# One matrix inverse per lane: three 128-partition transposes around it instead of ten 32-partition ones

## Chip, core and metric

The kernel runs on one core of a Trainium2 chip. The metric is the device time of one execution in microseconds. Five engines matter: TensorE (PE in the profile, with its weight loads as PEld), VectorE (DVE), ScalarE (ACT), GpSimd (POOL) and SyncE (SP, which issues most DMAs). Each engine works through its own queue in order.

## What is computed

The reference is a stack of two blocks on 256 tokens and 256 context positions, 1024 channels wide. First block: layer 0 is an RWKV-7 mixer with 32 heads of 64, run in both directions, and layer 1 a Hyena mixer. The second block has two layers of retention, spatial gating and differential attention. The change touches layer 0 alone. Its core is this scan, once forward and once in reverse, first over the context and then over the tokens:

```python
def rwkv7_scan(r, decay, k, v, kk, a, s0, reverse):
    xs = tuple(jnp.moveaxis(t.astype(jnp.float32), 1, 0) for t in (r, decay, k, v, -kk, kk * a))

    def step(s, inp):
        r_t, w_t, k_t, v_t, a_t, b_t = inp
        sa = jnp.einsum('bhvk,bhk->bhv', s, a_t)
        s = s * w_t[:, :, None, :] + sa[..., None] * b_t[:, :, None, :] + v_t[..., None] * k_t[:, :, None, :]
        return s, jnp.einsum('bhvk,bhk->bhv', s, r_t)

    s_last, ys = lax.scan(step, s0, xs, reverse=reverse)
    return jnp.moveaxis(ys, 0, 1), s_last
```

## The kernel before

**Chunks and groups.** The scan is done in chunks of 64 positions: 4 of the context and 4 of the tokens. Within a chunk, the term with `sa` is a triangular system, solved by multiplying with the inverse of a unit triangle of 64x64. There is one triangle for each chunk, head and direction. The heads go in 8 groups of 4, so that a group has 8 chunks x 4 heads x 2 directions = 64 triangles. Direction `z` 0 or 1 takes partitions 0 to 63 or 64 to 127, and the 32 blocks (chunk, head) lie along the free dimension.

**Steps of a group.** `rwkv_prep` (L842) makes the operands `AR`, `BK` and others from the projections, mostly on VectorE, ScalarE and GpSimd. `rwkv_inverse` (L936) makes the inverses `TT`. `rwkv_chain` (L1013) then runs the 8 chunks of either direction in order. One piece of the chain is a step of one direction: a right-hand side in PSUM (`ry`), ScalarE's copy of it (`RB`, L1076), the product with `TT` (`us`), ScalarE's copy `UV` (L1081), the state's update (`us` again, `St` L1092, `SB` L1094 and L1095 on GpSimd), and y. Beside that, `operands` prepares the next step's `qk` product, which VectorE masks into `ATT` (L1045). `rwkv_readout` closes a group.

**The inverse.** L941 to L955: 64 matmuls of 64x64x64 for a group (`mm`, L953, tile `pp`) make `AB`, copied out by ScalarE in four parts (L954). A 64x64 triangle consists of two diagonal 32x32 triangles and one off-diagonal block. L963 to L968: four transposes on VectorE (`nc.vector.transpose`, each 32 partitions by 1024 elements) bring the diagonal blocks into `LA` with one whole 32x32 matrix on each partition ("lane"). `lane_inverse` (L1111) inverts 32x32 triangles lane by lane with products and sums along the free dimension (`prod`, `mZ`, L1124 and L1125), VectorE for the most part, GpSimd for two of the products. L973 to L983: six more transposes of 32 partitions, four into `TT` (L980) and two into `T1` (L982). L985 to L1011: two rounds of 32x32 matmuls (`pi`) with ScalarE's copies (`XM` L996, `TT` L1010) give the off-diagonal block.

**Order.** While the chain of group g runs, each of its 16 pieces pulls along pieces of the inverse of g+1, of the preparation of g+2, of the read-out of g-1 and of the other layers' modulations (L816 to L821). The generators yield weights and `self.tot = [40, 51]` (L711) scales them: the inverse's weights are spread over 12 of the 16 pieces. That is the order in which the instructions are written; a planner (`schedule_with_timeline_sim=True`) then orders each engine's queue by its own model of times, and places the semaphores. Group 0's preparation and inverse come before the core, beside the projections of values and gates.

**Room.** Tiles of one tag share slots. `L` has three slots (`LA`, `X`, GpSimd's products, `T1`, `XM`); `prod` has one.

Of the kernel before, what the change touches and what calls it, by code (L numbers as in the profile page):

```python
# [31 lines left out]
# ---------------------------------------------------------------- constants of the shapes alone  # L32
def shape_constants():
# [24 lines left out]
    # filter embedding and window  # L58
# [32 lines left out]
    # second block: rotary tables and distances  # L91
# [24 lines left out]
class Parts:  # L116
    """K-tiles of an operand kept in several tiles of 4"""
# [9 lines left out]
class Net:  # L127
# [29 lines left out]
    def rstd(self, dst, ss, n, eps, pool):  # L157
        """dst = (ss / n + eps) ** -0.5; all [P, m]."""
        nc = self.nc
        sh = list(ss.shape)  # L160
        v = self.t(pool, sh, "rstd_v")
        nc.vector.tensor_scalar(v, ss, 1.0 / n, eps, ALU.mult, ALU.add)  # L162
        nc.gpsimd.tensor_tensor(dst, v, self.mhalf[:, 0:1].to_broadcast(sh), ALU.pow)  # L163

# [23 lines left out]
    def banks(self, n):  # L188
        """n banks for sums; after the first layer there are two of either tag, by turns"""
        if not self.two:  # L190
            return [self.t(self.ps, [128, 512], "mm") for _ in range(n)]
        tags = "mm", "x"
        self.bturn = 1 - self.bturn
        return [self.t(self.ps, [128, 512], tags[i // 2] if n > 2 else tags[self.bturn], bufs=2) for i in range(n)]

    def gemm_half_g(self, w, col0, nk, act, toks, evac):
        """the same for 512 columns in two halves, with two tiles of tokens in a bank: evac(i, psum, columns)"""
# [23 lines left out]
    def gemm_tok_g(self, w, col0, ncol, nk, act, toks, evac, tile_major=False):  # L221
        """token-major: psum[i] = act[:, toks[i]:+128]^T @ w[:, col0:+ncol]; a generator of pieces"""
# [33 lines left out]
    def gemm_ch(self, w, col0, ncol, nk, act, t0, nt, evac, side=None, raw=None):  # L256
        """channel-major: psum[c] = w[:, col0+128c:+128]^T @ act[:, t0:t0+nt]; side: a generator moved on by a
        piece after each load; raw: the first tile of w if it is loaded already"""
# [19 lines left out]
    def matvec(self, l, w, b, cols, gate_rows, rows, raws, scol, chunks=range(6), pool=None, tag="mm", width=512):  # L278
        """rows = silu(cond) @ w + b of modulation l for two conditions, in chunks of columns; shift and scale as
        columns into cols [128, 16, 2]; the gate parts go to DRAM rows {cond: dram[1, 1024]}; a generator of pieces"""  # L280
# [5 lines left out]
        for n, j in enumerate(chunks):  # L286
# [3 lines left out]
            for q in range(2):  # L290
                raw = vs[q] if vs else load(j, q)
                # each of the 4 K-tiles in a column group of its own
# [12 lines left out]
    def matvec_end(self, l, c0, row, b, cols, gate_rows, rows, pp, tag):  # L305
        """sums the column groups' rows and adds the bias"""
# [20 lines left out]
    def norm_split(self, xt, cols, cond, gcol, H, L, dt0, pool):  # L327
        """H + L [:, k, dt0:dt0+256] = (rms_norm(x) * g * (1 + scale) + shift)^T"""
# [28 lines left out]
    def transpose_split(self, src, n, H, L, k0, dt0, ntok=2, half=False):  # L357
        """src (or half of it) token-major [128, ntok, n*128] -> H/L [:, k0+k, dt0:dt0+128*ntok]"""
# [16 lines left out]
    def residual(self, act, nk, w, streams, post, pool, done=None, side=None):  # L375
        """for every stream (old, new, gate row, first token): new = old + gate * rms_norm(act^T @ w, post);
        done(stream, tile, columns) after each part of the last; side() comes before the last K tiles"""
# [37 lines left out]
        if nk == 16:  # L415
            # the last K tiles may come late
# [22 lines left out]
        else:  # L439
            # all the weights at hand, one tile of tokens after the other  # L440
# [15 lines left out]
    def setup(self):  # L456
# [9 lines left out]
        # sums the four column groups' rows  # L466
# [3 lines left out]
    def pack_rows(self, rows, tag, pool, tmp, eng=None, ptag="mm"):  # L470
        """rows: DRAM views [n, 128]; returns [128, sum n] of their transposes"""
# [14 lines left out]
    def rwkv_project(self):  # L486
# [17 lines left out]
        # per-channel parameters as columns  # L504
# [5 lines left out]
        # silu of both blocks' conditions, [K-tile, row], the rows from 2 on zero  # L510
# [8 lines left out]
        # the tokens take the place of d until they are normalised and transposed; order: context, tokens  # L519
# [41 lines left out]
        # d = shifted - h; context: channels < 512 from the previous token, others from the next one  # L561
# [33 lines left out]
        def lerp_g(g, t0, nt, pool, tag, out, every=3):  # L595
            """out = the parts of h + mu d; gives way after each half of the channels"""
# [32 lines left out]
        # the gate of this layer's modulation, in tiles that the bottlenecks leave  # L629
# [4 lines left out]
        # k, and 1 / max(norm, 1e-12) of k * k_k per head  # L634
# [4 lines left out]
        for j in range(4):  # L639
# [9 lines left out]
            if j == 0:  # L649
                # decay and in-context-rate bottlenecks by direction, [parts x 64, tokens]  # L650
# [20 lines left out]
        # to DRAM by head; the rows lie at 32 (pair mod 4) + 2 (pair div 4) + half  # L671
# [39 lines left out]
        self.tot = [40, 51]  # L711
# [12 lines left out]
    def set(self, es):  # L724
        """room for the operands of one more group"""
# [4 lines left out]
    def operand(self, g, n, shape, tag):  # L730
        """group g's tile in the first n sets by turns"""
        return self.t(self.sets[g % n], shape, tag)

    def rwkv_open(self):
        """what the preparation needs"""
# [11 lines left out]
        # sigmoid(v) = (1 + tanh(v / 2)) / 2; k_dir = k (1 + (a - 1) k_a)  # L747
# [8 lines left out]
        # entries off the valid blocks stay zero  # L756
# [8 lines left out]
    def rwkv_core(self):  # L765
# [8 lines left out]
        # operands of the even and the odd heads of the pairs, the other heads' rows zero  # L774
# [8 lines left out]
        # the other layers' modulations, in the gaps  # L783
# [19 lines left out]
        for g in range(G):  # L803
# [7 lines left out]
            if g == G - 2:  # L811
                # the filters take the room of the third set and of the modulations
# [12 lines left out]
        # the rest goes into the gaps before the next layer  # L825
# [6 lines left out]
    def advance(self, gen, amount):  # L832
        """emit pieces of gen until their weights reach amount"""
# [8 lines left out]
    def rwkv_prep(self, g, s):  # L842
        """operands of the 4 heads of group g for both directions"""
# [3 lines left out]
        # [two copies of 64, z, w2 | a2, channel]: the product with both parts of the bottleneck at once  # L847
# [15 lines left out]
        for p in range(2):  # L863
# [6 lines left out]
            # negated normalised key direction  # L870
# [6 lines left out]
            for z in range(2):  # L877
# [16 lines left out]
                # a <- -sigmoid  # L894
# [32 lines left out]
            # bonus weights sum_k r k_dir r_k per token and head  # L927
# [8 lines left out]
    def rwkv_inverse(self, g, s):  # L936
        """inverses of the chunks' triangles"""
# [3 lines left out]
        # A_ab^T of every chunk: rows (z, s), [block (chunk, head), t]; entries outside the triangle are not read  # L941
        AB = self.t(self.abp[g % 2], [128, 32, 64], "AB")
        ABv = AB.rearrange("p (c i j) t -> p c i j t", i=2, j=2)
        for hf in range(2):
            for j in range(2):
                jr = slice(64 * j, 64 * j + 64)
                q = self.t(ps, [128, 512], "pp")
                for cc in range(4):
                    for i in range(2):
                        for z in range(2):  # L950
                            o = 128 * cc + 64 * i
                            ra = AR[z][1][jr, i, cc, 0] if hf else AR[z][0][jr, i, cc]
                            mm(q[64 * z:64 * z + 64, o:o + 64], BK[z][hf][jr, i, cc, 0], ra, True, True)  # L953
# [3 lines left out]
        # unit-lower inverses of the 32x32 diagonal blocks, one block per lane  # L957
# [4 lines left out]
        nc.gpsimd.memset(Xt[:, 0:1024:33], 1.0)  # L962
        for z in range(2):  # L963
            for hf in range(2):
                q0 = 64 * z + 32 * hf
                src = AB[q0:q0 + 32, :, 32 * hf:32 * hf + 32].rearrange("p b t -> p t b")
                dst = LA[q0:q0 + 32]
                nc.vector.transpose(dst if z == 0 else dst.rearrange("p s t -> p t s"), src)  # L968
        yield 4
        yield from self.lane_inverse(p1, LAt, Xt)  # L970

        s["TT"] = TT = self.TTs[g % 2]
# [941 lines left out]
```

## Time and profile before

| | |
|---|---|
| median of 3 runs | 2575.11 us (2574.1 to 2586.33) |
| span of the profiled execution | 2584.2 us |
| busy PE, DVE, ACT, POOL | 92%, 62%, 46%, 32% |
| layer 0's core (first chain to last) | about 404 to 1262 us |
| mean granted TensorE clock | 0.944 of full speed |

A busy share of the page is a mean over stages with different limits. The core is one stage of nearly 900 us in which neither PE nor DVE is full on the mean. It has a period of 104 to 112 us, one group, and is read period by period.

### The profile page before, as it was taken

What the parts mean: (1) busy time and instruction counts of PE and PEld (TensorE: products, weight loads), DVE (VectorE), ACT (ScalarE), POOL (GpSimd) and SP (SyncE); (2) the same over time, 40 slices, a digit from 0 to 9 for tenths busy, and PEclk for the clock granted to TensorE, in tenths of its full rate; (3) what the DMA queues carried; (4) which work ended last, traced back from release to release, by engine and by line L of the source; (5) the groups of instructions that cost most, each with busy time, mean ns of one, the idle gap of its engine ahead of it and who ended that gap; (6) DMA issues with size and microseconds to landing.
All of it is one profiled execution on the core that took longest, in us unless ns stands there. A gap on an engine that the chain in (4) does not pass through costs nothing. (4 is left out here: it accounts for less than half of the span.)

```text
span 2584.2 us, 43519 instructions
## 1 busy us (share of the span) xinstructions
PE 2377.7 (92%) x17635; PEld 1995.9 (77%) x17635; DVE 1595.8 (62%) x2238; ACT 1201.3 (46%) x2238; POOL 834.1 (32%) x800
## 2 busy tenths in 40 slices
PE   6999977788888888979899999999999999999998
PEld 4578866667676666767779998788899987888886
DVE  6564495967779687694457676653345634654464
ACT  4345464564655646545335444433235623433453
POOL 4233342554545445442112333120022111121231
PEclk9999986987888989899999999999999999999999
DMA  6546441232232332204446554332222132344333
GB/s 216 199 141 193 159 156 44 87 116 83 88 111 86 96 103 84 64 27 148 141 146 201 166 165 162 110 114 82 82 79 86 52 122 82 119 130 133 100 130 131
DMA packets 203757, 305.82 MB, mean 118 GB/s; under 512 B 12593, under 2 KB 110542, under 8 KB 203556
## 3 DMA queue, kind: packets, MB, share of 16 engines
q1 hardware_dynamic: 194528, 276.08, 33.1%
q0 software_dynamic: 6096, 19.77, 2.1%
q10 hardware_dynamic: 2932, 7.18, 0.9%
q8 instruction: 139, 2.28, 0.4%
q14 instruction: 62, 0.51, 0.1%
HBM read 281.93 MB, written 21.06 MB: 117 GB/s over the span
## 5 line engine op out<-in xcount | busy, mean ns | idle before, releaser
L155 DVE TENSOR_TENSOR wlo<-wraw,whi 128x2048 fp32r<-128x2048 f32 (+1 forms) x156 | 364.5, 2338 | 315.6 <-ACT whi L154 315.4
L154 ACT CAST whi<-wraw 128x2048 fp32r<-128x2048 f32 (+1 forms) x172 | 321.8, 1874 | 299.9 <-PE x L151 149.5
L151 PE MATMUL mm<-whi,hH 128*128 128x256 f32 (+1 forms) x944 | 303.0, 324 | 5.4 <-ACT rs_junk L399 2.3
L151 PE MATMUL mm<-wlo,hH 128*128 128x256 f32 (+1 forms) x944 | 302.2, 321 | 0.0
L151 PE MATMUL mm<-whi,hL 128*128 128x256 f32 (+1 forms) x944 | 300.8, 320 | 0.0
L151 PEld LDWEIGHTS mm<-whi,hH 128*128 128x128 f32 x944 | 179.8, 191 | 20.3 <-ACT rs_junk L399 2.8
L151 PEld LDWEIGHTS mm<-wlo,hH 128*128 128x128 f32 x944 | 180.0, 191 | 14.3 <-POOL wlo L155 0.2
L151 PEld LDWEIGHTS mm<-whi,hL 128*128 128x128 f32 x944 | 179.6, 190 | 14.2 <-DVE hL L355 0.2
L1045 DVE TENSOR_TENSOR ATT<-qk,mask 128x512 f32<-128x512 f32 (+1 forms) x128 | 70.4, 551 | 117.6 <-PE qk L151 72.0
L151 PE MATMUL x<-wlo,hH 128*128 128x512 f32 x352 | 141.4, 402 | 0.7 <-POOL wlo L155 0.7
L151 PE MATMUL x<-whi,hH 128*128 128x512 f32 x352 | 138.8, 401 | 1.9 <-ACT whi L154 1.9
L151 PE MATMUL x<-whi,hL 128*128 128x512 f32 x352 | 140.3, 401 | 0.0
L151 PE MATMUL ry<-UV,ATT 128*64 128x64 f32 x1536 | 139.5, 240 | 0.6 <-ACT UV L1081 0.6
L155 POOL TENSOR_TENSOR wlo<-wraw,whi 128x2048 fp32r<-128x2048 f32 x16 | 73.5, 4594 | 201.7 <-ACT whi L154 201.7
L151 PEld LDWEIGHTS ry<-UV,ATT 128*64 128x64 f32 x1536 | 116.2, 149 | 21.4 <-issue 6.7
L1094 POOL TENSOR_TENSOR St<-St,SB 128x256 f32<-128x256 f32 x84 | 76.0, 905 | 152.8 <-ACT St L1092 140.6
L151 PE MATMUL qk<-PD,BKx 128*128 128x256 f32 x256 | 81.9, 447 | 19.5 <-DVE ATT L1045 18.5
L1124 DVE TENSOR_TENSOR prod<-L,L 128x512 f32<-128x512 f32 (+8 forms) x88 | 96.3, 1094 | 0.9
L151 PE MATMUL us<-RB,TT 128*64 128x64 f32 x1024 | 93.0, 239 | 2.6 <-ACT RB L1076 2.4
L151 PEld LDWEIGHTS us<-RB,TT 128*64 128x64 f32 x1024 | 76.1, 149 | 22.7 <-issue 7.5
L151 PE MATMUL us<-UV,BKt 128*128 128x128 f32 x448 | 80.1, 305 | 8.0 <-ACT UV L1081 7.8
L1095 POOL TENSOR_TENSOR SB<-St,PC 128x256 f32<-128x256 f32 x98 | 72.6, 742 | 36.4 <-ACT St L1092 31.9
(562 smaller groups left out, 6451.1 us busy)
## 6 DMA issues: line engine op xcount, KB each, us to landing
wraw<-in_w_in SPq DMA_DIRECT2D x68, 1024.0 KB
wraw<-in_l_w_in SPq DMA_DIRECT2D x64, 1024.0 KB
raw<-in_w_mod SPq DMA_DIRECT2D x48, 512.0 KB
wraw<-in_w_out SPq DMA_DIRECT2D x24, 1024.0 KB
raw<-in_ada_w SPq DMA_DIRECT2D x24, 512.0 KB
wraw<-in_w_branch_out SPq DMA_DIRECT2D x12, 1024.0 KB
UV<-vD SPq DMA_DIRECT2D x128, 64.0 KB
lH<-in_ada_w SPq DMA_DIRECT2D x5, 1024.0 KB
```

The source lines that it names most:

```text
L151: return self.nc.tensor.matmul(out, lhsT, rhs, start=start, stop=stop)
L154: self.nc.scalar.copy(hi, src)
L155: (eng or self.nc.vector).tensor_tensor(lo, src, hi.bitcast(F32), ALU.subtract)
L1045: nc.vector.tensor_tensor(at.rearrange("p i j a t -> p (i j) (a t)"), q[:, 0:256 * na].rearrange("p (h n) -> p h n", h=4), mk, ALU.mult)
L1094: nc.gpsimd.tensor_tensor(tmp, tmp, SB[z][step % 2], ALU.add)
L1095: nc.gpsimd.tensor_tensor(SB[z][1 - step % 2], tmp, pc, ALU.mult)
L1124: eng.tensor_tensor(pr, a, b, ALU.mult)
```

## The change

Three edits in `rwkv_inverse`, and one number beside it (most other lines of the full diff only drop comments).

- The matmuls that make `AB` are split and rearranged, so that for both directions and both halves the diagonal block stands in columns 0 to 31 and the off-diagonal one in columns 32 to 63, with rows and columns exchanged for direction 1. One matmul of a chunk, head and direction becomes two (direction 0) or three (direction 1): 160 for a group instead of 64, each with 32 columns of weights.
- One transpose of 128 partitions replaces four of 32 ahead of `lane_inverse`.
- Two transposes of 128 partitions (`XT[0]` into a slot of `L`, `XT[1]` into the slot of `prod`) replace six of 32 behind it. ScalarE copies the diagonal blocks from them into `TT` with four copies of 32 partitions by 1024 elements. The `pi` matmuls read `XT` in the place of `T1` and of the diagonal blocks of `TT`.
- The yields' weights sum to 43.2 instead of 46.2, and the total they are scaled by is 46 instead of 51.

```diff
-        self.tot = [40, 51]
+        self.tot = [40, 46]
...
-                            ra = AR[z][1][jr, i, cc, 0] if hf else AR[z][0][jr, i, cc]
-                            mm(q[64 * z:64 * z + 64, o:o + 64], BK[z][hf][jr, i, cc, 0], ra, True, True)
+                            a = AR[z][1][jr, i, cc, 0] if hf else AR[z][0][jr, i, cc]
+                            b = BK[z][hf][jr, i, cc, 0]
+                            lo, hi = slice(0, 32), slice(32, 64)
+                            r0, r1 = q[64 * z:64 * z + 32], q[64 * z + 32:64 * z + 64]
+                            if z == 0:
+                                mm(r0[:, o:o + 64], b[:, lo], a, True, True)
+                                mm(r1[:, o:o + 64].rearrange("p (x y) -> p x y", y=32), b[:, hi], a.rearrange("p (x y) -> p x y", y=32)[:, ::-1], True, True)
+                            else:
+                                mm(r0[:, o:o + 64], a[:, lo], b, True, True)
+                                mm(r1[:, o:o + 32], a[:, hi], b[:, hi], True, True)
+                                mm(r1[:, o + 32:o + 64], b[:, hi], a[:, lo], True, True)
...
-        for z in range(2):
-            for hf in range(2):
-                q0 = 64 * z + 32 * hf
-                src = AB[q0:q0 + 32, :, 32 * hf:32 * hf + 32].rearrange("p b t -> p t b")
-                dst = LA[q0:q0 + 32]
-                nc.vector.transpose(dst if z == 0 else dst.rearrange("p s t -> p t s"), src)
-        yield 4
+        nc.vector.transpose(LA, AB[:, :, 0:32].rearrange("p b t -> p t b"))
+        yield 2
         yield from self.lane_inverse(p1, LAt, Xt)
...
-        T1 = self.t(p1, [128, 1056], "L", bufs=3)[:, 0:1024].rearrange("p (a b) -> p a b", b=32)
+        XT = []
+        for n, src in enumerate((X, X.rearrange("p a b -> p b a"))):
+            x = self.t(p1, [128, 1056], "L", bufs=3)[:, 0:1024] if n == 0 else self.t(p1, [128, 1024], "prod")
+            x = x.rearrange("p (b s) -> p b s", s=32)
+            nc.vector.transpose(x.rearrange("p b s -> p s b"), src)
+            XT.append(x)
+            yield 2
         for z in range(2):
             for hf in range(2):
                 q0 = 64 * z + 32 * hf
-                rows = X[q0:q0 + 32]                      # z = 0: (t, s); z = 1: (s, t)
-                alt = rows.rearrange("p a b -> p b a")
-                dst = TT[q0:q0 + 32, :, 32 * hf:32 * hf + 32].rearrange("p b t -> p t b")
-                nc.vector.transpose(dst, rows if z == 0 else alt)
-                if hf == z:
-                    nc.vector.transpose(T1[q0:q0 + 32].rearrange("p b s -> p s b"), alt if z == 0 else rows)
-            yield 3
+                nc.scalar.copy(TT[q0:q0 + 32, :, 32 * hf:32 * hf + 32], XT[z][q0:q0 + 32])
+        yield 1
...
-                    mm(q[b0:b0 + 32, 32 * j:32 * j + 32], AB[a0:a0 + 32, b, b0 - 64 * z:b0 - 64 * z + 32], T1[a0:a0 + 32, b, :], True, True)
+                    mm(q[b0:b0 + 32, 32 * j:32 * j + 32], AB[a0:a0 + 32, b, 32:64], XT[1 - z][a0:a0 + 32, b, :], True, True)
...
-                    mm(q[a0:a0 + 32, 32 * j:32 * j + 32], XM[b0:b0 + 32, b, :], TT[b0:b0 + 32, b, bt:bt + 32], True, True)
+                    mm(q[a0:a0 + 32, 32 * j:32 * j + 32], XM[b0:b0 + 32, b, :], XT[z][b0:b0 + 32, b, :], True, True)
```

## Rows read from the trace of the kernel before

**Rows 1.** The page, part 1: busy us, share of the span, instructions.
```profile
PE 2377.7 (92%) x17635; PEld 1995.9 (77%) x17635; DVE 1595.8 (62%) x2238; ACT 1201.3 (46%) x2238; POOL 834.1 (32%) x800
```

**Rows 2.** Stretches: us; busy PE, PEld, DVE, ACT, POOL (instructions); clock, DMA, GB/s.
```profile
388.00:444.00 56.00, 44.55 (x527) 39.42 (x526) 28.05 (x33) 26.01 (x58) 15.04 (x18) 0.58 0.10 31
444.00:556.00 112.00, 93.65 (x1096) 74.73 (x1096) 91.23 (x118) 67.37 (x161) 57.33 (x63) 0.94 0.33 103
556.00:668.00 112.00, 98.07 (x1019) 76.78 (x1019) 81.81 (x110) 59.07 (x143) 55.13 (x59) 0.82 0.30 93
884.00:988.00 104.00, 86.47 (x988) 68.82 (x989) 81.68 (x113) 58.74 (x141) 52.79 (x59) 0.90 0.29 91
1092.00:1164.00 72.00, 58.64 (x548) 46.97 (x548) 65.18 (x79) 32.26 (x88) 37.32 (x35) 0.94 0.11 33
1262.00:2584.20 1322.20, 1278.03 (x7828) 1133.22 (x7828) 710.03 (x1119) 543.05 (x857) 295.42 (x219) 0.98 0.37 122
```

**Rows 3.** The same view, two periods cut in two, a third's first part.
```profile
444.00:516.00 72.00, 55.78 (x499) 42.88 (x498) 70.30 (x85) 40.10 (x97) 38.30 (x41) 0.93 0.29 93
516.00:556.00 40.00, 37.87 (x598) 31.85 (x599) 20.93 (x34) 27.27 (x64) 19.02 (x23) 0.96 0.41 120
556.00:628.00 72.00, 58.07 (x502) 42.68 (x502) 71.38 (x93) 38.75 (x92) 42.46 (x44) 0.87 0.34 105
628.00:668.00 40.00, 40.00 (x521) 34.10 (x520) 10.43 (x18) 20.32 (x51) 12.67 (x15) 0.72 0.25 71
884.00:956.00 72.00, 54.48 (x485) 41.44 (x486) 71.51 (x88) 39.10 (x92) 41.27 (x45) 0.92 0.25 80
```

**Rows 4.** Timeline of DVE in one period: start, us, instruction, [idle before, releaser].
```profile
549.50 8.31 DVE L968 STREAM_TRANSPOSE L<-AB 32x1024 f32<-32x1024 f32 x4 [2.30 <-ACT AB L954]
...
612.09 1.98 DVE L980 STREAM_TRANSPOSE TT<-L 32x1024 f32<-32x1024 f32 x1
...
615.98 5.85 DVE L980 STREAM_TRANSPOSE TT<-L 32x1024 f32<-32x1024 f32 x3
621.73 1.86 DVE L982 STREAM_TRANSPOSE L<-L 32x1024 f32<-32x1024 f32 x1
```

**Rows 5.** Groups by form, DVE, 300 to 1264: count | busy us, mean ns | idle before.
```profile
L968 DVE STREAM_TRANSPOSE L<-AB 32x1024 f32<-32x1024 f32 x32 | 66.3, 2073 | 5.3 <-ACT AB L954 4.8
L980 DVE STREAM_TRANSPOSE TT<-L 32x1024 f32<-32x1024 f32 x32 | 64.4, 2011 | 0.6
...
L982 DVE STREAM_TRANSPOSE L<-L 32x1024 f32<-32x1024 f32 x16 | 30.9, 1930 | 0.0
```

**Rows 6.** Who PE waited for, 444 to 1164: total us, times, longest.
```profile
PE qk L1050 <- DVE ATT L1045: 21.1, 11, 4.1
PE qk L151 <- DVE ATT L1045: 19.3, 12, 2.9
PE pi L151 <- DVE L L982: 16.5, 8, 3.9
```

**Rows 7.** Timeline of PE: the inverse's matmuls.
```profile
403.68 1.91 PE L151 MATMUL pi<-L,AB 32*32 32x32 f32 x32 [5.61 <-DVE L L982]
...
521.40 2.11 PE L151 MATMUL pi<-L,AB 32*32 32x32 f32 x64
...
627.68 3.43 PE L151 MATMUL pi<-L,AB 32*32 32x32 f32 x64
```

**Rows 8.** Timeline of PE: small matmuls in a row (the last cut at four).
```profile
538.00 1.15 PE L151 MATMUL pp<-ARc,BKc 64*64 64x64 f32 x32 [0.64 <-ACT mv L301]
...
540.83 0.63 PE L151 MATMUL ry<-UV,ATT 128*64 128x64 f32 x8
...
590.88 0.42 PE L151 MATMUL pp<-raw,scol 128*32 128x256 f32 x4
```

**Rows 9.** ACT: two copies by form, and the timeline behind the first `pi` matmuls.
```profile
L954 ACT COPY AB<-pp 128x512 f32<-128x512 f32 x32 | 18.7, 585 | 18.0 <-PE pp L151 17.9
...
L1010 ACT COPY TT<-pi 32x512 f32<-32x512 f32 x32 | 18.4, 576 | 23.4 <-PE pi L151 23.2
...
625.59 1.16 ACT L996 COPY L<-pi 32x512 f32<-32x512 f32 x2 [4.32 <-PE pi L151]
```

More of the change, by code (lines that the diff above doesn't have):

```diff
@@ L962, in rwkv_inverse @@
         nc.gpsimd.memset(Xt[:, 0:1024:33], 1.0)
+        nc.vector.transpose(LA, AB[:, :, 0:32].rearrange("p b t -> p t b"))
+        yield 2
+        yield from self.lane_inverse(p1, LAt, Xt)
+        s["TT"] = TT = self.TTs[g % 2]
+        XT = []
[5 more added lines that the diff above has]
+            yield 2
         for z in range(2):
@@ L965, in rwkv_inverse @@
                 q0 = 64 * z + 32 * hf
-                src = AB[q0:q0 + 32, :, 32 * hf:32 * hf + 32].rearrange("p b t -> p t b")
-                dst = LA[q0:q0 + 32]
-                nc.vector.transpose(dst if z == 0 else dst.rearrange("p s t -> p t s"), src)
-        yield 4
-        yield from self.lane_inverse(p1, LAt, Xt)
-        s["TT"] = TT = self.TTs[g % 2]
-        T1 = self.t(p1, [128, 1056], "L", bufs=3)[:, 0:1024].rearrange("p (a b) -> p a b", b=32)
-        for z in range(2):
-            for hf in range(2):
-                q0 = 64 * z + 32 * hf
-                rows = X[q0:q0 + 32]
-                alt = rows.rearrange("p a b -> p b a")
-                dst = TT[q0:q0 + 32, :, 32 * hf:32 * hf + 32].rearrange("p b t -> p t b")
-                nc.vector.transpose(dst, rows if z == 0 else alt)
-                if hf == z:
-                    nc.vector.transpose(T1[q0:q0 + 32].rearrange("p b s -> p s b"), alt if z == 0 else rows)
-            yield 3
+                nc.scalar.copy(TT[q0:q0 + 32, :, 32 * hf:32 * hf + 32], XT[z][q0:q0 + 32])
+        yield 1
         XM = self.t(p1, [128, 1056], "L", bufs=3)[:, 0:1024].rearrange("p (a b) -> p a b", b=32)
@@ L1002, in rwkv_inverse @@
                 b0 = 64 * z + 32 * (1 - z)
-                bt = b0 - 64 * z
                 for j in range(16):
                     b = 16 * hb + j
-                    mm(q[a0:a0 + 32, 32 * j:32 * j + 32], XM[b0:b0 + 32, b, :], TT[b0:b0 + 32, b, bt:bt + 32], True, True)
+                    mm(q[a0:a0 + 32, 32 * j:32 * j + 32], XM[b0:b0 + 32, b, :], XT[z][b0:b0 + 32, b, :], True, True)
             for z in range(2):
```

## The prediction

> **What bounds the kernel now.** I read the page first [rows 1]: PE 92% busy, DVE 62%. By that mean DVE looks free and a change that gives PE more instructions looks bad. The stretches tell more. Behind 1262 us PE is busy for 1278 of 1322 us [rows 2]; nothing of the change runs there, so that half stays. Layer 0's core is another matter: its periods of 104 to 112 us have PE at 83 to 88% and DVE at 73 to 81%, neither full. Cutting periods in two shows why [rows 3]. In the first 72 us DVE is full (70.3, 71.4, 71.5 of 72) and PE is busy for 55.8, 58.1 and 54.5, so it idles for 14 to 18 us. In the other 40 us PE is full (37.9, 40.0) and DVE half idle or more. Two engines bound the core by turns. The first part begins with the inverse's four transposes and ends with the other six [rows 4]; the lane inverse, the next group's preparation and the chain's masks lie between. The second holds the `pi` matmuls, the end of one chain, the start of the next, and the matmuls for the next `AB`.
>
> The periods close a loop: `TT` lets the next chain begin, the next `AB` is made beside that chain's first pieces, its transposes wait for it (2.30 us idle ahead of them [rows 4]), and the lane inverse and six transposes lead to `pi` and the next `TT`. All ten transposes lie in the part that DVE sets. PE's waits agree: 21.1 + 19.3 us for DVE's masks and 16.5 us for the last transposes [rows 6].
>
> **Part 1, transposes.** A group has 4 x 2.073 + 4 x 2.011 + 2 x 1.930 = 20.2 us of them now [rows 5]. Three of 128 partitions follow. No row shows a transpose of 128 partitions. From above: four quarters one after the other, 4 x 2.02 = 8.1 us each. From below: the same 1024 elements on each partition as now, about 2.02 us; less than that is excluded, since the length in elements is the same. I take 2.02, because on ACT copies of 32x512 and 128x512 take 0.576 and 0.585 us [rows 9]: there time goes by elements, not by partitions, and that is the nearest comparison. So 3 x 2.02 = 6.1 and DVE gets back 14.1 us a group: 6.2 ahead of the lane inverse, 7.9 behind it.
>
> The Trainium skill, "Vector Engine (DVE) Microarchitecture Reference", section 3.8, puts a 32x32 reorder array ahead of each bank of 32 channels and says that it sustains one element per cycle and lane. The first half is for 2.02 us and no run here shows it. The second, with 0.96 GHz from "VectorE: DVE Perf Modes" (Specifications), would make 1.07 us for 1024 elements (an estimate); the rows show 1.93 to 2.07, so the measurement decides. By the page's rate three would be 3.2 us, 2.9 us a group more than I count.
>
> **Part 2, matmuls of AB.** 64 now run as 32 in 1.15 us, some 30 ns each at full clock [rows 8]: two column groups at a time, 60 ns for a pair. A pair becomes a set of five in four column groups of 32. Four matmuls in four column groups take 0.42 us together [rows 8], so groups of 32 do run side by side; then a set lasts as long as its longest column group. One matmul of 64 columns takes 0.63 / 8, less the tail, about 58 ns; two of 32 columns in one group take 2 x 32 = 64 (64 `pi` in 2.11 us [rows 7]). 64 instead of 60 ns x 32 sets is 0.1 us a group. From above: no overlap, 3 x 58 + 2 x 32 = 238 ns, 5.7 us a group. Between: no long row of small matmuls shows less than 30 ns a start, and 5 x 30 = 150 ns would be 2.9 us a group. A gain is excluded: no column group streams fewer columns than now. I take 0.1, since the four side by side have the new shape of weights. Eight groups: 1 us; 23 or 46 at the bounds. They lie in the part that PE sets, so all of it would count.
>
> The Trainium skill, "TensorEngine Tiling (Array Packing)", section Instruction Overhead, speaks against this split: each matmul costs some 60 cycles however short it is, and a dimension already small should not be cut. At full clock that is 25 ns (an estimate), 125 for a set, 2.1 us a group and 17 in all.
>
> **Part 3, copies into TT.** Four ACT copies of 32x1024 a group. From above twice a 32x512 [rows 9], 1.15 us; from below one, 0.58. I take 1.1, elements setting the time: 4.4 us a group on ACT. They queue from the first `XT` on, ahead of the copies of `pi` (L996) and among the chain's copies. `pi` reads `XT` and doesn't wait for them; the next chain needs `TT`, but its off-diagonal copies come later anyway. Their cover is the 4.32 us in which ACT waited for `pi` [rows 9]; without it up to 4.4 us a group come onto the path. I count 0.1, for both.
>
> **Part 4, slots and weights.** `XT[1]` holds the only `prod` slot until the second `pi` round. The next lane inverse, DVE's next user, stands behind the next `AB` and its transposes: from 538.00, the first of those matmuls, to 557.81, the end of the transposes [rows 4, 8], that is 20 us of cover; without it DVE would stop at its first product with the masks queued behind. `L` keeps its count of tiles. The weights end the inverse at 43.2 / 46 x 12 = 11.3 instead of 46.2 / 51 x 12 = 10.9 of 16 pieces, 0.4 x 7 = 2.8 us later in the written order, nothing where data sets the start, as at 549.50. No DMA moves.
>
> **The sum.** For a steady group: PE's work in the first part stays at (55.8 + 58.1 + 54.5) / 3 = 56.1 us. Without 14.1 us the part would be 57.9, with PE at 97%. I don't believe that, since the chain's steps pass through ACT and POOL. The fullest whole period has PE at 98.07 / 112 = 88% [rows 2]. With 88% the part is 56.1 / 0.88 = 63.8: a gain of 8.2, less 0.2 for parts 2 and 3, so 8.0. What stalls next is PE waiting for the chain's copies and GpSimd's state. Seven such groups: 56 us. Group 0's inverse comes ahead of the first chain; there PE waits 5.61 us at a time for the last transposes [rows 7] and is 80% busy at a clock of 0.58 [rows 2], so nearly all comes back: 12 of 14.1. Together 68 us, from 2584.2 to 2516 for the profiled execution; that one is 9 us above the median, so 2575.1 - 68 = 2507. Own range 2483 to 2539 (PE in that part at 93% or at 82%).
>
> **Rivals.**
> 1. *All of it and the clock too.* 8 x 14.1 = 113 us come back: 2462. Behind the transposes `pi` ran at half speed, 64 in 3.43 against 2.11 us [rows 7], after PE had waited; 628 to 668 had a clock of 0.72, so 22 of 40 us at half [rows 3]. With shorter waits some 5 us a group more: 2425. Against it: PE would need 97% or more. Chance 0.15, most of it between 2460 and 2480.
> 2. *Spacing.* PE starts no small matmul each 30 ns or faster in the long run (the Trainium skill's overhead, above, says nearly the same). Then 2507 + 23 = 2530. For: no row below 30. Against: four in 0.42 us. Chance 0.10.
> 3. *PE and ACT take it back.* PE cannot work denser in the first part because its gaps are the chain's latency. Then only PE's idle share there, 22% of 14.1 = 3.1 us a group, comes back: 12 + 22 = 34, 2541; with the spacing or half the copies' cover lost 2564. For: ACT and GpSimd stand in every step. Against: 57 us of PE's waits name DVE [rows 6]. Chance 0.15.
> 4. *Slower.* The transpose of 128 partitions passes its quarters one after the other, on DVE at either end of the lane inverse: 3 x 8.1 = 24.2 against 20.2 us, 4 us a group, 32 in all: 2607. It decides from 20.2 / 3 = 6.7 us for one. Chance 0.06. Then the change would not do what it says.
> 5. *Another order.* The planner, with other lengths, puts long VectorE instructions ahead of the masks: 4.4 us a group lost instead of won, 2590 and more. Chance 0.04.
>
> **How the numbers follow.** Forecast 0.50, rivals 0.15, 0.10, 0.15, 0.06, 0.04. About 0.5%, 13 us, is what a measurement tells from no change: faster is below 2562. Faster 0.50 + 0.15 + 0.10 + 0.09 = 0.84; same 0.06 (the upper end of rival 3); slower 0.10. The range from 2462 to 2560 leaves out some of rival 1, the end of rival 3, and rivals 4 and 5.
>
> **What would show it.** Right: 24 transposes of some 2 us; DVE-full parts of 60 to 66 instead of 72 us with PE near 88%; sets of five in 60 to 70 ns; the stretch behind the core unchanged. Wrong: transposes over 6 us; `AB` matmuls of 32 sets in 5 us or more for a group; ACT's copies of `pi` queued behind the new copies; PE's idle time in the DVE part now named after ACT or GpSimd.

## The result, and the profile after

The changed kernel takes 2556.3 us (median of eight executions) where the kernel before, measured again beside it, takes 2576.9: ratio 0.9893, interval 0.9866 to 0.9921. That is 27 us faster, between 20 and 35. Forecast were 68, so the sign and the range held and the size was two and a half times too large. In this document a difference of one point in the ratio stands for 25.8 us.

First, part 1 of the page of the kernel after (busy us, share of the span, instructions):

```profile
span 2557.6 us, 46534 instructions
PE 2366.6 (93%) x19171; PEld 1992.6 (78%) x19171; DVE 1508.1 (59%) x2182; ACT 1232.6 (48%) x2270; POOL 831.7 (33%) x800
```

Against [rows 1], DVE is busy 87.7 us less, though the transposes alone give back 114 (161.6 us in [rows 5], 47.6 below): something else on DVE grew by 26 us. ACT has 31 us more. The groups of the inverse by form (count | busy us, mean ns | idle before them, and what ended it), layer 0 of the kernel after:

```profile
L984 DVE STREAM_TRANSPOSE prod<-L 128x1024 f32<-128x1024 f32 x8 | 16.0, 1999 | 0.0
L974 DVE STREAM_TRANSPOSE L<-AB 128x1024 f32<-128x1024 f32 x8 | 15.8, 1971 | 9.6 <-ACT AB L965 9.6
L984 DVE STREAM_TRANSPOSE L<-L 128x1024 f32<-128x1024 f32 x8 | 15.8, 1971 | 0.1
L990 ACT COPY TT<-L 32x1024 f32<-32x1024 f32 x16 | 16.7, 1046 | 6.3 <-DVE L L984 6.2
L990 ACT COPY TT<-prod 32x1024 f32<-32x1024 f32 x16 | 16.6, 1040 | 0.2
```

A transpose of 128 partitions takes what one of 32 took, 1.97 to 2.00 us. A copy takes 1.04. Both are close to the values taken in the prediction, 2.02 and 1.1. So neither was mis-sized, and the missing time is not in their durations. Where it is not saved is seen from the period. The next rows give the first transposes of each group: before (four a group; the last group's set is the second row, from DVE's timeline) and after (one a group), with first and last start.

```profile
L968 DVE STREAM_TRANSPOSE L<-AB x28: 1933/2050/2196, 441.6 to 1101.0; 32x1024 f32<-32x1024 f32 x28
...
1094.89 8.23 DVE L968 STREAM_TRANSPOSE L<-AB 32x1024 f32<-32x1024 f32 x4 [1.26 <-ACT AB L954]
```

```profile
L974 DVE STREAM_TRANSPOSE L<-AB x7: 1910/1969/2018, 431.4 to 1074.2; 128x1024 f32<-128x1024 f32 x7
```

Group 0's part gave back 441.6 - 431.4 = 10.2 us, where 12 were forecast. The six periods between first and last set went from (1094.9 - 441.6) / 6 = 108.9 to (1074.2 - 431.4) / 6 = 107.1 us: 1.8 a group instead of 8.0 (a second profile of the kernel after, 430.0 to 1065.2, has 105.9, so 3.0). The shortfall is in the steady groups.

The stretches of the kernel after, as in [rows 2, 3] (us; busy PE, PEld, DVE, ACT, POOL; clock, DMA, GB/s): two periods cut in two, a third's first part, and what lies behind the core:

```profile
433.00:484.00 51.00, 41.86 (x321) 30.93 (x321) 48.79 (x64) 28.14 (x68) 28.34 (x27) 0.87 0.27 85
484.00:540.00 56.00, 51.23 (x949) 42.66 (x949) 25.62 (x47) 38.88 (x89) 27.35 (x35) 0.95 0.41 126
540.00:594.00 54.00, 36.97 (x272) 29.02 (x272) 52.01 (x64) 25.46 (x58) 26.64 (x25) 0.82 0.20 61
594.00:653.00 59.00, 55.70 (x956) 44.96 (x955) 24.84 (x43) 41.44 (x98) 27.08 (x36) 0.92 0.42 124
653.00:712.00 59.00, 46.80 (x338) 35.23 (x338) 56.13 (x69) 32.52 (x75) 34.09 (x34) 0.83 0.24 70
...
1240.00:2557.60 1317.60, 1274.21 (x7826) 1130.20 (x7826) 709.48 (x1118) 543.12 (x857) 294.74 (x219) 0.98 0.38 123
```

The parts in which DVE is full did get shorter, 51 to 59 us instead of 72; the forecast was 63.8. But PE is busy for only 82%, 68% and 79% of them, 77% together, where it had been 78% in [rows 3] and the forecast was 88%. PE did not get denser beside a full DVE: its busy share there did not rise. The work that it did not do there (42, 37 and 47 us instead of 56) came in the parts that PE fills, which grew from 40 to 56 and 59 us. The whole period has PE where it was, at 82 to 87%. Behind the core PE is busy for 1274 of 1318 us; nothing changed there, as forecast.

Who PE waited for in the core of the kernel after, 433 to 1153 (total us, times, longest), beside [rows 6]:

```profile
PE qk L1057 <- DVE ATT L1052: 22.9, 12, 4.9
PE qk L151 <- DVE ATT L1052: 21.7, 7, 6.1
PE ry L151 <- POOL SB L1102: 19.3, 18, 3.2
...
PE pi L151 <- DVE prod L984: 2.8, 3, 1.8
```

The wait for the last transposes went from 16.5 to 2.8 us. The wait for the masks, 21.1 + 19.3 = 40.4 us before, is 44.6 after: the freed time on DVE did not reach it. The wait for GpSimd's state stands third with 19.3 (13.3 before).

### The profile page after: what moved, and what is told of

Same layout as the page of the kernel before. It is cut to its first block, busy times and chain, and to the rows that moved or that the text cites. A ratio compares the mean times of both kernels' runs of the same rounds, so it can differ in the third digit from the quotient of the medians.

```text
span 2557.6 us, 46534 instructions
## 1 busy us (share of the span) xinstructions
PE 2366.6 (93%) x19171; PEld 1992.6 (78%) x19171; DVE 1508.1 (59%) x2182; ACT 1232.6 (48%) x2270; POOL 831.7 (33%) x800
## 5 line engine op out<-in xcount | busy, mean ns | idle before, releaser
L1102 POOL TENSOR_TENSOR SB<-St,PC 128x256 f32<-128x256 f32 x98 | 81.6, 833 | 17.2 <-ACT St L1099 13.3
L1083 ACT COPY RB<-ry 64x256 f32<-64x256 f32 x128 | 46.7, 365 | 82.7 <-PE ry L151 81.0
```

What stands on the lines that cost most here:

```text
L1083: nc.scalar.copy(rhs[zr], ry[0:64, 0:256])
L1102: nc.gpsimd.tensor_tensor(SB[z][1 - step % 2], tmp, pc, ALU.mult)
```

## Experiments

Ratios are to the kernel before, with 95% intervals. Differences between two changed kernels are taken from their ratios, their bounds from both intervals. Where nothing else is said, the edit is made in the kernel after.

**The same kernel again, and the old total.** One run repeats the kernel after; the other puts the total of the weights back:

```diff
-        self.tot = [40, 46]
+        self.tot = [40, 51]
```

> The changed kernel again, unaltered, beside the next three on one chip. Both theories: a ratio of 0.989, within 0.986 to 0.993 of the kernel before.

> The changed kernel with the old total of the weights, 51 in the place of 46, so that the inverse is written earlier beside the chain. Theory A (in the changed kernel the chain of a group follows on the chain before at once, its last UV copy to the next first one 0 to 3 us, and TT is ready 10 to 15 us too early; the chain and TensorE set the pace, the time of VectorE no longer does): an inverse that is written earlier gains nothing, 2550 to 2565. Theory C (the planner's order gave the gain away, and 46 is part of that): over 10 us of difference either way, below 2545 or above 2570.

Measured: 0.9905 (0.9875 to 0.9935) and 0.9918 (0.9884 to 0.9952). The gain repeats, and the total does not make it or spoil it.

**DVE's time given back to it.** The transposes are written several times, four of the first and three each of the other two: ten a group, as before.

```diff
-        nc.vector.transpose(LA, AB[:, :, 0:32].rearrange("p b t -> p t b"))
+        for _ in range(4):
+            nc.vector.transpose(LA, AB[:, :, 0:32].rearrange("p b t -> p t b"))
...
-            nc.vector.transpose(x.rearrange("p b s -> p s b"), src)
+            for _ in range(3):
+                nc.vector.transpose(x.rearrange("p b s -> p s b"), src)
```

> The changed kernel with each transposition done again, the first one four times, the two others three times each: ten transposes a group as before, 14 us a group of VectorE time put back, all else as changed. Theory A (what was gained is the part of VectorE's time that the chain did not cover, and the new matmuls and copies cost nothing): back to the time of before, 2570 to 2585. Theory B (VectorE's time was worth some 60 us, and the 160 matmuls and the four copies took 40 of it back): above the time of before by what they cost, 2600 or more.

Measured: 1.0147 (1.0092 to 1.0202). This splits the change in two. Without the saved DVE time it is 38 us slower than before (24 to 52): that is what all the rest of it costs, in the order that the planner chose for this run. The saved DVE time is worth the difference to the kernel after, 65 us (49 to 81), with the same reservation. The prediction had 69 for it (7 x 8.2 + 12) and about 1.5 for the rest.

**One end of it alone.** The first transpose written four times (the first edit above; 5.9 us a group, 47 in all), and the two behind the lane inverse left out:

```diff
-        for n, src in enumerate((X, X.rearrange("p a b -> p b a"))):
...
+        for n in range(2):
+            XT.append(X)
```

> The changed kernel with the transposition ahead of the lane inverse done four times: 3 x 1.97 = 5.9 us a group of VectorE put back, 47 us in all. Theory B (a microsecond of VectorE is worth 0.4 to 0.6 on the whole way between the kernels): 19 to 28 us slower than the changed kernel, ratio 0.997 to 1.001. Theory K (a knee: near the changed kernel the chain sets the pace, and VectorE's time is free): within 8 us of the changed kernel, ratio 0.987 to 0.993.

> The changed kernel without the two transpositions behind the lane inverse; the matrices are used as they lie, so that layer 0's recurrence is computed with wrong inverses. 2 x 2.0 = 4 us a group of VectorE fewer, 32 us in all, and pi starts 4 us earlier behind the lane inverse. Theory B: 13 to 19 us faster than the changed kernel, ratio 0.982 to 0.985. Theory K: within 8 us, ratio 0.987 to 0.993.

Measured: 1.0042 (1.0011 to 1.0072), 38 us more than the kernel after for 47 us of DVE (28 to 49), above both theories; and 0.9847 (0.9798 to 0.9895), 12 us less for 32 (between 27 less and 3 more). So transposes added to DVE cost 0.8 us per us here and 65 / 111 = 0.6 with all ten. What further time taken off DVE would bring is not settled by the second run.

**In what form the time comes.** The core of six runs, one profiled execution of each, from 400 us to the end of the last chain (us; busy PE, PEld, DVE, ACT, POOL; clock, DMA, GB/s): the kernel before, the kernel after, all transposes repeated, the first one four times, and two runs told below, the split matmuls alone in the kernel before and the kernel after without its four copies:

```profile
400.00:1261.00 861.00, 748.49 (x8013) 594.29 (x8013) 632.84 (x844) 470.85 (x1128) 385.55 (x415) 0.88 0.28 87
400.00:1238.00 838.00, 733.44 (x9229) 586.72 (x9227) 553.50 (x788) 492.42 (x1146) 387.28 (x412) 0.89 0.29 90
400.00:1304.00 904.00, 775.62 (x9367) 623.05 (x9366) 623.47 (x840) 501.73 (x1158) 394.00 (x414) 0.85 0.27 83
400.00:1269.00 869.00, 768.14 (x9325) 607.71 (x9324) 574.67 (x811) 496.83 (x1155) 392.92 (x412) 0.86 0.28 87
400.00:1291.00 891.00, 775.84 (x9357) 617.53 (x9358) 637.25 (x845) 472.11 (x1130) 389.64 (x415) 0.85 0.28 85
400.00:1219.00 819.00, 716.51 (x9192) 572.85 (x9191) 552.32 (x789) 464.57 (x1120) 391.66 (x412) 0.91 0.30 92
```

What PE waits is the length less its busy time: 113 us before, 105 after. With all transposes repeated it is 128, 24 more than after; the other 42 of the 66 us are PE busy for longer at a lower granted clock. With the first transpose four times PE waits 101 us, no more than after: all 31 us are busy time. The split (30 us longer in this execution, the longest of its ten) adds 27 us of busy time and 3 of waiting; leaving out the copies takes off 17 and 2. Busy time multiplied by the clock is 652 to 661 us in all six, so the matmuls' work hardly differs; how much of it ran at the lower of TensorE's two levels does. The clock of whole executions says the same: 0.930 to 0.943 in the ten with the first transpose four times, 0.944 to 0.955 in the eight of the kernel after. What made the clock fall is not shown by any run here.

**The split matmuls alone, in the kernel before.** Weights of 32 columns, 160 for a group; transposes, slots and copies as before:

```diff
-                            mm(q[64 * z:64 * z + 64, o:o + 64], BK[z][hf][jr, i, cc, 0], ra, True, True)
+                            mm(r0[:, o:o + 64], b[:, lo], ra, True, True)
+                            if z == 0:
+                                mm(r1[:, o:o + 64], b[:, hi], ra, True, True)
+                            else:
+                                mm(r1[:, o + 32:o + 64], b[:, hi], ra[:, hi], True, True)
+                                mm(r1[:, o:o + 32], b[:, hi], ra[:, lo], True, True)
```

> The kernel before with its 64 matmuls for AB split into 160 of 32 columns of weights, in the same five-in-a-set pattern as in the change, the layout of AB and all else as before. Priced by the trace of the changed kernel (80 matmuls in 1.22 us against 32 in 1.15): theory A 0.1 us a group, no difference, 2570 to 2585. Theory B: 17 to 46 us slower, 2594 to 2623.

Measured: 1.0045 (1.0011 to 1.0079), 12 us slower (3 to 20). Its rows on PE's timeline (start, us), half a group at half and at full clock:

```profile
543.20 1.93 PE L151 MATMUL pp<-ARc,BKc 64*32 64x64 f32 x80
...
664.86 1.22 PE L151 MATMUL pp<-ARc,BKc 64*32 64x64 f32 x80
```

80 matmuls in 1.22 us at full clock, against 32 in 1.15 [rows 8]: 15 ns each, 0.14 us a group, 1.1 us in all. Sets of five do run side by side, and rival 2's spacing of 30 ns is out. So of the 12 us, which lie between the two theories, the matmuls themselves are one. The rows above show the rest as a lower clock. That it comes from the order into which the planner puts 96 more instructions is likely and not shown; the next two runs show how much another order can be.

**Order alone, in the kernel before.** No instruction differs; the weights are scaled otherwise, so that pieces are written in other places.

```diff
-        self.tot = [40, 51]
+        self.tot = [40, 46]
```

```diff
-        self.tot = [40, 51]
+        self.tot = [44, 51]
```

> The kernel before with the total 46 in the place of 51: every instruction and every duration as before, the written order of the inverse against the chain later. It shows how much the planner's order alone moves the time. Theory C (the order's scatter is as large as the 12 and 16 us put down to matmuls and copies): over 10 us either way. Theories A and B: within 8 us of before.

> The kernel before with the preparation's total 44 in the place of 40: every instruction as before, another written order. A second sample of what the order alone does, beside +0.3 points from the inverse's total. Theory C (the 0.45 points of the split matmuls are order): 0.4 points or more either way. Theory B (they are the matmuls): within 0.3 points of 1.

Measured: 1.0027 (0.9997 to 1.0056) and 1.0068 (1.0037 to 1.0098): 7 (not clear of zero) and 18 us slower with the same instructions. The 12 us of the split lie within what another order does. Whether the split has a price beyond it stays open.

**The four copies left out.**

```diff
-        for z in range(2):
-            for hf in range(2):
-                q0 = 64 * z + 32 * hf
-                nc.scalar.copy(TT[q0:q0 + 32, :, 32 * hf:32 * hf + 32], XT[z][q0:q0 + 32])
```

> The changed kernel without ScalarE's four copies of the diagonal blocks into TT, so that this part of TT stays zero and the recurrence of layer 0 is computed with half of the inverse only. 4 x 1.04 us of ScalarE a group fall away. Theory A: hidden behind waits for TensorE, 0 to 5 us faster, 2551 to 2557. Theory B: they stand in the chain's queue, 4 us a group come back, 20 to 35 us faster, 2520 to 2537.

Measured: 0.9832 (0.9776 to 0.9889), 16 us less than the kernel after (0 to 32). Taken out of the version with the state on VectorE (below) they bring 12 us (1 to 23):

> The changed kernel with the state's update on VectorE and without ScalarE's four copies into TT (part of TT stays zero, layer 0's recurrence is computed with half of the inverse). With the state on GpSimd their removal brought 0.6 points. Theory B (ScalarE's queue in the chain: each us of it costs): again 0.5 points or more, ratio 0.972 to 0.977. Theory C (that was another order of the planner): ratio 0.979 to 0.985.

Measured: 0.9766 (0.9736 to 0.9796), against 0.9812. The two agree on some 14 us, 1.7 a group, where the prediction counted 0.1. But leaving out instructions also changes the order, which alone moved the kernel before by 7 and 18 us, so 14 us is not shown to be the copies' own price. ACT's timeline of the kernel after shows the place (start, us, instruction):

```profile
592.07 2.10 ACT L990 COPY TT<-L 32x1024 f32<-32x1024 f32 x2
594.20 0.72 ACT L891 ACTIVATE F<-F,one 128x512 f32<-128x512 f32 x1
594.82 0.35 ACT L1099 COPY St<-us 128x256 f32<-128x256 f32 x1
595.08 0.37 ACT L1059 COPY BKt<-qk 128x256 f32<-128x256 f32 x1
595.47 2.09 ACT L990 COPY TT<-prod 32x1024 f32<-32x1024 f32 x2
597.59 0.37 ACT L1115 COPY Y<-ry 64x256 f32<-64x256 f32 x1
597.98 0.37 ACT L1088 COPY UV<-us 64x256 f32<-64x256 f32 x1
598.37 0.69 ACT L889 ACTIVATE a<-pp,wah 128x512 f32<-128x512 f32 x1
599.09 1.17 ACT L1004 COPY L<-pi 32x512 f32<-32x512 f32 x2
```

None of these rows has idle time ahead of it. The running chain's `St` stands behind the first pair of copies, its `UV` behind the second, the `pi` copies behind both. The copies did fill the time in which ACT had waited for `pi` (36.1 us in the core before, 8.8 after), but the chain's copies come through the same queue: between two steps of a chain ACT must be free when `us` is done. Without the copies the same place runs so:

```profile
587.24 0.36 ACT L1095 COPY St<-us 128x256 f32<-128x256 f32 x1
587.50 0.39 ACT L1055 COPY BKt<-qk 128x256 f32<-128x256 f32 x1
...
588.53 0.37 ACT L1111 COPY Y<-ry 64x256 f32<-64x256 f32 x1
588.92 0.37 ACT L1084 COPY UV<-us 64x256 f32<-64x256 f32 x1
```

From `St` to `UV` it takes 1.7 us instead of 3.2. So the delay of the chain is seen. How it becomes time is not the same in the two runs: here PE waits only 2 us less in the whole core, while in the version with the state on VectorE leaving the copies out took 12 us off PE's waiting (86 to 73).

**The copies on GpSimd** instead of ScalarE:

```diff
-                nc.scalar.copy(TT[q0:q0 + 32, :, 32 * hf:32 * hf + 32], XT[z][q0:q0 + 32])
+                nc.gpsimd.tensor_copy(TT[q0:q0 + 32, :, 32 * hf:32 * hf + 32], XT[z][q0:q0 + 32])
```

> The changed kernel with the four copies of the diagonal blocks on GpSimd instead of ScalarE. Theory B (the copies cost 16 us because they stand in ScalarE's queue ahead of the chain's copies): most of it comes back, 2540 to 2550, ratio 0.983 to 0.987, as without them, unless GpSimd's state update waits behind them. Theory A (the copies cost nothing, what their removal showed is another order): as the changed kernel, 2552 to 2565, or above.

Measured: 1.0178 (1.0152 to 1.0204), 73 us worse than on ScalarE, which neither theory told. GpSimd is the emptiest of the engines by the page, and a worse place than ScalarE. Why it costs so much was not taken apart; the four copies themselves take 1.2 us each there, 4.8 us a group.

**The state on VectorE.** If GpSimd's state is what PE waits for next, and DVE now has room, the two should be exchanged. The chain already has the other branch for the last group; it is used for all:

```diff
-                    if g < 7:
+                    if g < 0:
```

> The changed kernel with the state's update of all groups on VectorE (two instructions of some 0.42 and 0.46 us that read PSUM) instead of one ScalarE copy (0.37) and two GpSimd instructions (0.97 and 0.84): the chain of a step gets 1.3 us shorter, VectorE gets 12.3 us a group more, nearly what the transposes gave back, ScalarE 5.2 less. Theory A (the chain's latency now sets the period): up to 7 x 1.3 = 9 us a group less, 2490 to 2535, ratio 0.965 to 0.982. Theory B (a microsecond of VectorE in a group is still worth 0.58, as the repeated transposes showed, and the chain's latency is hidden behind the other direction's work): 12.3 x 0.58 x 7 = 50 us more, less 10 to 20 for ScalarE: 2580 to 2600, ratio 1.00 to 1.01.

> The kernel before with the state's update on VectorE in all groups, as in the run before on the changed kernel, where that brought 0.9 points. Theory A (before, VectorE and the chain's latency are both full; only the change made the room that the shorter chain needs): 12.3 us a group more on a full VectorE eats the gain, ratio 0.995 to 1.015. Theory D (the chain's latency alone sets the pace, before as after): the same 0.9 points, ratio 0.988 to 0.994.

Measured: in the kernel after 0.9812 (0.9781 to 0.9842), 21 us less than the change alone (10 to 32); in the kernel before 1.0335 (1.0299 to 1.0371), 86 us more, beyond both theories. The same edit has opposite signs, and the change decides which. PE's waits of the kernel before with it, 444 to 1200, and then of the kernel after with it, 433 to 1140:

```profile
PE pi L151 <- DVE L L982: 36.0, 9, 6.3
PE ry L151 <- DVE SB L1101: 30.4, 17, 4.1
```

```profile
PE ry L151 <- DVE SB L1108: 20.1, 17, 3.5
PE qk L1057 <- DVE ATT L1052: 11.3, 14, 1.6
PE qk L151 <- DVE ATT L1052: 8.4, 6, 4.2
```

Before, on an engine without room, the `pi` wait doubles (16.5 to 36.0 us) and the state's wait grows as well (13.3 to 30.4). After, the masks' wait falls from 44.6 to 19.7 us although DVE has more instructions. With the copies on VectorE as well (`nc.vector.tensor_copy` in their line):

> The changed kernel with the state's update and the four copies into TT on VectorE. ScalarE loses 4.2 us a group more, VectorE gets four copies of 32x1024, 0.6 to 1.1 us each. Theory B: ScalarE's part is worth 12 to 16 us, VectorE's 2.4 to 4.4 us a group at 0.5 cost 8 to 16: between 0.977 and 0.983 of the kernel before. Theory K (VectorE's time is free by now): 0.975 to 0.979.

Measured: 0.9799 (0.9738 to 0.9861), not to be told from the 0.9812. The two are the best versions found that compute the whole inverse, some 2% below the kernel before.

**The inverse spread over 15 instead of 12 of the 16 pieces**, in the kernel after and with the state on VectorE:

```diff
-                side.append([self.rwkv_inverse(g + 1, st[g + 1]), tot[1], 0, 12])
+                side.append([self.rwkv_inverse(g + 1, st[g + 1]), tot[1], 0, 15])
```

> The changed kernel with the inverse's pieces spread over 15 of the chain's 16 pieces instead of 12. Theory A (TT comes 10 to 15 us before it is needed, the inverse is off the loop): VectorE's work is spread more evenly, the masks wait less, 0 to 15 us faster than the changed kernel, ratio 0.984 to 0.990. If the inverse is still what the next chain waits for: later by up to 3 pieces of 6.7 us in a group, slower than the changed kernel, ratio 0.995 or more.

> The changed kernel with the state's update on VectorE and the inverse over 15 pieces. Theory A: in the run with the state on VectorE, TT came 6 us ahead of its use (620 against 625 us), so there is little left to give: within 8 us of that run, ratio 0.978 to 0.985. If the inverse comes onto the loop: 0.988 or more.

Measured: 0.9958 (0.9935 to 0.998) and 0.988 (0.9846 to 0.9913): 17 us worse both times. A later inverse is no gain. That fits a `TT` without time to spare, but 17 us is also what another order alone has moved.

## Why the prediction was right or wrong

*What bounds the kernel.* Right for the kernel before: DVE and PE bound the core by turns, and the stretch behind the core is untouched. The part that DVE fills got shorter by 13 to 21 us, about all that the transposes gave back.

*The step that failed* is the sum's step from DVE's part to the period. It kept PE's work in that part at 56.1 us and let PE do it at 88% instead of 78%, so that 8.2 of 14.1 us would come back. Measured are 77%, as dense as before, and 42, 37 and 47 us of work; the rest of the work moved into the other part. PE's waiting in the core fell by 8 us, from 113 to 105, where the forecast had 57 in the seven steady groups. A steady group gained 1.8 us (3.0 in the second profile).

*Rival 3* had this: PE does not get denser there, and only its idle share of the freed time comes back, 3.1 us a group and 34 in all. Measured are 27, and its time, 2541 to 2564, came true. The repeated transposes bear out its price as well: for 111 us put back on DVE PE waited 24 us more, a fifth. They cost 65 because PE's busy time grew at a lower clock, and that the rival does not price. Its reason, the chain's latency, is not shown by itself; that the state on VectorE, a shorter chain, brought 21 us, and that PE waits 86 us in its core instead of 105, speaks for it.

*Part 1 and its conversion.* The durations were right: 1.97 to 2.00 us a transpose against 2.02. Group 0 gave 10.2 us against 12. The 65 us lie near the 69 of the sum by luck: the sum priced PE's waiting, and 42 of the 66 us in the rows are clock. Rival 4, quartered transposes, is out by the durations. Rival 1's gain did not come; its clock moved both ways, to 0.87, 0.82 and 0.83 from 0.93, 0.87 and 0.92 where DVE is full, and to 0.95 and 0.92 from 0.96 and 0.72 where PE is. Rival 5, another order, did not come as it was told (no loss), but order as a cost did; its 2590 does not follow from 4.4 us a group, which make 31 us in seven groups, or 2606.

*Parts 2 and 3* at 0.2 us a group together were the other mis-sized term. Against that stand 38 us (24 to 52) for everything but the saved DVE time.
- Part 3: the durations were right (4 x 1.04 against 4.4 us), the cover was not. The prediction set 4.4 us of copies against 4.32 us of ACT's waiting for `pi`, found the room exactly full, and then counted it as free; its own bound was 4.4 us a group. The copies stand ahead of the chain's and of the `pi` copies, a sign that it had named for being wrong. Leaving them out measured 14 us, 1.7 a group, which lies within what order moves.
- Part 2's own price was right (0.14 us a group against 0.1). That 96 more instructions a group may move the order was not priced. The split alone measured 12 us (3 to 20), and a changed order without any changed instruction 7 and 18.
- The other 12 of the 38 us are not assigned. The slots of part 4 and the order of the finished change are in them; no run separates those. The weights' total is not the cause: with 51 in the place of 46 the ratio is the same.

No term of the sum was for the clock. With the transposes repeated PE is busy for 27 us more than in the kernel before and waits 16 more. Whether the order, the copies or the split lowers the clock stays open.

*What stalls next.* The prediction named the chain's copies and GpSimd's state. The rows show both: the copies above, the state with 19.3 us. It missed that the masks' wait would stay (40.4 to 44.6 us). They were most of the 57 us that the prediction held against rival 3; that a wait names an engine did not mean that time freed on the engine would reach that wait.

*The range* reached to 2560 through rival 3 and held; the forecast's own range, 2483 to 2539, did not. Its lower bound on PE's density, 82%, was above the 78% that its own rows showed. The chance of 0.15 for rival 3 was too low for that.

## What to carry to other kernels

When a full engine gets shorter, do not let the other engine get denser beside it without a reason: take the density that the rows show, and count as gain only its idle share of the freed time. Split a measured difference into the other engine's waiting and its busy time with the granted clock beside it; here several runs differed mostly in the second. When work moves from a full engine to one with gaps, ask of each gap which chain step it belongs to: a gap as long as the work may be no cover if the next link of a latency chain comes through the same queue. Price the order too: under a planner, a change of weights alone moved this kernel by 0.7% once and by 0.3%, not clear of zero, another time, so an edit "worth nothing" carries an uncertainty of about that. And once a bottleneck engine has room, try again what was put elsewhere to relieve it: the state's update lost 3.4% on VectorE before the change and won 0.8% after it.

## What the runs showed of the hardware

VectorE's instructions grew while its work shrank. One line by form, in layer 0 of the kernels before, after, and after with the state on VectorE (count | busy us, mean ns | idle before):

```profile
L906 DVE TENSOR_TENSOR kd<-kd,K 128x512 f32<-128x512 f32 x28 | 24.2, 864 | 1.3 <-ACT kd L893 1.3
```

```profile
L906 DVE TENSOR_TENSOR kd<-kd,K 128x512 f32<-128x512 f32 x28 | 35.3, 1262 | 1.7 <-ACT kd L893 1.7
```

```profile
L906 DVE TENSOR_TENSOR kd<-kd,K 128x512 f32<-128x512 f32 x28 | 23.1, 824 | 2.7 <-ACT kd L893 2.6
```

The same instruction with the same operands differs by half in the mean. The timelines of DVE and POOL in the kernel after show one that took 3.38 us, and that of the version with the state on VectorE one that took 0.68:

```profile
569.95 3.38 DVE L906 TENSOR_TENSOR kd<-kd,K 128x512 f32<-128x512 f32 x1
...
569.90 2.89 POOL L1131 TENSOR_TENSOR L<-L,mZ 128x1024 f32<-128x1024 f32 x1 [2.29 <-DVE mZ L1132]
```

```profile
560.31 0.68 DVE L906 TENSOR_TENSOR kd<-kd,K 128x512 f32<-128x512 f32 x1
```

GpSimd's product began 0.05 us ahead of `kd` and ended at 572.79; `kd` ended 0.54 us later, close to its own length. It looks like waiting, and counts as busy. The Trainium skill, "SBUF — State Buffer", section "SBUF: two separate sides", says that a VectorE operation with two SBUF inputs and a GpSimd operation that reads SBUF share a port pair under an exclusive lock, held for the whole instruction by whoever starts first; these rows agree. So do the others of this line: 14 of its 32 products in the kernel after took over 0.9 us, with GpSimd busy beside them for 1.5 of their 1.8 us on the mean; beside the 18 others, of 0.7 us, it was busy for 0.14. The page of the version with the state on VectorE, which leaves GpSimd less work, fits too:

```profile
PE 2354.2 (93%) x19171; PEld 1983.2 (79%) x19171; DVE 1525.0 (60%) x2364; ACT 1205.8 (48%) x2172; POOL 687.8 (27%) x618
```

GpSimd gave up 144 us, and DVE took 182 instructions more, 90 us by their rows less some 11 that the last group had anyway; yet DVE's busy time rose by 17 us only. The durations of all its other instructions together fell by some 46 us; the rest is overlap of instructions that follow each other. The lock would also be a reason for the 26 us by which the rest of DVE grew under the change, which was not tested by itself. It is no reason for the 38 us of everything but the saved DVE time: in the run with the transposes repeated the growth is gone. The page there:

```profile
PE 2400.3 (91%) x19171; PEld 2020.6 (77%) x19171; DVE 1588.3 (61%) x2238; ACT 1233.9 (47%) x2270; POOL 841.0 (32%) x800
```

Of DVE's 1588.3 us 159 are transposes; the rest, 1429, is no more than the 1434 of the kernel before.
